# The pairs' weight sums: from sums on VectorE and GpSimd to transfers that add

## The chip, the cores and the metric

The kernel runs on one core of a Trainium2 chip. The core has five engines: TensorE (PE) multiplies matrices, VectorE (DVE) and ScalarE (ACT) work element by element, GpSimd (POOL) does general work and may issue transfers, and SyncE (SP) issues transfers. Sixteen DMA engines move data between DRAM and the on-chip memory. The metric is the time of one execution on the device in microseconds (us); less is better.

## What is computed

One layer of a hybrid sequence mixer over 16 learned tokens and 512 rows of width 2048, in float32:

```
u    = rms_norm(h, g_norm)
proj = u @ w_in                      # eight parts of 1024 columns: rq rk rv rg dq dk dv dg
r    = retention(rq, rk, rv)         # 8 heads of 128
r    = head_layer_norm(r) * silu(rg)
d    = diff_attention(dq, dk, dv)    # 8 heads, two softmaxes each
d    = head_rms_norm(d) * (1 - lam_init) * silu(dg)
out  = rms_norm(h + concat(r, d) @ w_out)
```

So each head needs eight column blocks of `w_in`, each 2048 x 128.

## The kernel before, in words

**Precision.** A float32 operand is split into a high part (rounded to the matmul's type by ScalarE) and a low part (operand minus high part, by VectorE). A product is then three matmuls: high x high, high x low, low x high.

**Start.** The rows of x are normalised, transposed and split into four quarters: `ua` (first half of the tokens, all 16 row tiles of D), `uc` and `ud` (second half, first and last eight row tiles). The first head's parts rv, rq, rk, rg, dv, dk are projected directly (`first_two`, `project`). Beside that, `sums_of_u` (L724 to L754) makes four signed sums of the quarters, `sums[1..4]`: `whole` joins high and low parts on GpSimd (L733), `out` splits a sum again (L736 to L738).

**Pairs.** The other 29 pairs of column blocks (`pair_list`: rv with rk, rq with rg, dv with dk, dq with dg) go through `run_pair`. A pair (ka, kb) is a product of a 2 x 2 block matrix of u with a 2 x 2 block matrix of weights: b11 and b21 are the two halves of ka, b12 and b22 those of kb, each 128 x 1024 in the buffer (512 KB). It is done with seven products in place of eight (Winograd's form of Strassen's scheme): P1 with b11, P2 with b21, P3 with b22, and four with sums of blocks: P7 with b22 - b12, P6 with b22 - b12 + b11, P5 with b12 - b11, P4 with b21 less the P6 sum. Each product is 24 matmuls (L813): 16 with the high part of the weights, 8 with the low part.

**Weights of a pair.** `load_pair` issues four loads (`raw_tile`, L94) into a ring of five buffers (`wr`). In DRAM a block's row is 128 numbers long, 512 B, so a load is 1024 pieces. `prepare_hi` copies the high part on ScalarE (L785), `prepare_lo` makes the low part on VectorE (L796) and then makes the next sum in place, over the buffer that was just read: after P3 on VectorE (L799), after P7 on VectorE (L801), after P1 two on GpSimd (L803, L804). The order of the products is P3, P7, P1, P6, P2, P5, P4. Product i runs while the parts of product i + 2 are prepared; there are three buffers each for high (`wh`) and low (`wl`) parts.

**Between the products** the work of heads that are already projected goes on by steps: `ret_task` (scores, decay, output), `diff_task` (two softmaxes per block, transposes, output), and `finish`, which normalises a head's output. In `finish` a row of sums goes by DMA over the partitions (`mc`, L467), through four small GpSimd steps (`rc`, L469 to L472), to DRAM (`rd`, L474) and back to all partitions (`sq`, L476); VectorE then multiplies (L479).

**Order.** After the start a scheduler of the framework orders the instructions of each engine at build time by its own estimate of durations; on the chip each engine works its list in order and waits on semaphores. A transfer belongs to the list of the engine that issues it: SyncE before the change, apart from the last stores.

**Output.** Five column chunks of `w_out` follow (L980 on), with the residual and the last norm.

Of the kernel before, what the change touches and what calls it, by code (L numbers as in the profile page):

```python
# [39 lines left out]
def hymba_kernel(ctx: ExitStack, tc: tile.TileContext, x, meta, norm_g, w_in, w_out, g_ret, g_diff,  # L40
# [27 lines left out]
    w_in_t, w_out_t = (w.rearrange("(k p) n -> p k n", p=P) for w in (w_in, w_out))  # L68

    def w_piece(name, h, half):  # L70
        c0 = OFFSETS[name] + h * P
        return w_in_t[:, half * 8:half * 8 + 8, c0:c0 + P]
# [622 lines left out]
    def put_dk(src):  # L695

        a = kbuf[0]
        for (d1, cols), (d2, _) in zip(*(both_parts(a[:, i, :]) for i in range(2))):
            act.copy(out=d1, in_=src[:, :, cols])
            vec.tensor_tensor(out=d2, in0=src[:, :, cols], in1=f(d1), op=ALU.subtract)  # L700
        return spread_dk()
# [22 lines left out]
    def sums_of_u():  # L724
# [3 lines left out]
        for k in range(0, 8, 2):  # L728
# [7 lines left out]
            def out(i, t):  # L736
                act.copy(out=sums[i][0][:, sl, :], in_=t)
                vec.tensor_tensor(out=sums[i][1][:, sl, :], in0=t, in1=f(sums[i][0][:, sl, :]), op=ALU.subtract)  # L738
# [3 lines left out]
            vec.tensor_tensor(out=d, in0=c, in1=d, op=ALU.add)  # L742
            out(1, d)
# [8 lines left out]
            vec.tensor_tensor(out=a2, in0=a2, in1=d, op=ALU.subtract)  # L752
            out(4, a2)
            yield  # L754

# [11 lines left out]
    ORDER = ("P3", "P7", "P1", "P6", "P2", "P5", "P4")  # L767
# [3 lines left out]
    def load_pair(n):  # L771
        if n < len(pair_list) and n not in raw_w:
            h, ka, kb = pair_list[n]
            raw_w[n] = {b: raw_tile(w_piece(k, h, half), P, f"{b}_{n}")
                        for b, k, half in (("b22", kb, 1), ("b12", kb, 0), ("b11", ka, 0), ("b21", ka, 1))}

    SOURCE = {"P3": "b22", "P7": "b22", "P1": "b11", "P6": "b22", "P2": "b21", "P5": "b12", "P4": "b11"}
# [10 lines left out]
    def prepare_lo(i):  # L788
# [9 lines left out]
        if pn == "P3":  # L798
            vec.tensor_tensor(out=w["b22"], in0=w["b22"], in1=w["b12"], op=ALU.subtract)  # L799
        elif pn == "P7":  # L800
            vec.tensor_tensor(out=w["b22"], in0=w["b22"], in1=w["b11"], op=ALU.add)  # L801
        elif pn == "P1":
            pool.tensor_tensor(out=w["b12"], in0=w["b12"], in1=w["b11"], op=ALU.subtract)  # L803
            pool.tensor_tensor(out=w["b11"], in0=w["b21"], in1=w["b22"], op=ALU.subtract)  # L804
# [11 lines left out]
    def run_pair(n, T):  # L816
# [19 lines left out]
        s37 = ap.tile([P, 2, HL], F32, tag="s37", name=f"s37_{nm}")[:, :, :w]  # L836
        p3 = pj(f"p3_{nm}")[:, :w]
        run(0, p3)
        snap(p3, None, s37[:, 0, :])
        step()  # L840
        v = pj(f"v_{nm}")[:, :w]
        run(1, v)
        snap(v, None, s37[:, 1, :])
# [276 lines left out]
```

## Time and profile before

| what | value |
|---|---|
| median of 3 runs | 1031.96 us (1031.91 to 1035.21) |
| the profiled execution | 1036.45 us |
| its span, first to last instruction | 1034.4 us |
| TensorE / VectorE / ScalarE / GpSimd busy | 93% / 80% / 52% / 23% of the span |
| mean granted clock of TensorE | 0.983 of full speed |
| transfers | 127.03 MB, mean 123 GB/s |

The page comes from the profiled execution. A busy share is an average over stages with different limits. Matmuls are pipelined, so a matmul's own duration (about 0.28 us) is longer than the distance to the next. Times in the trace count from the start of the span. Register, branch, semaphore and DMA-issuing instructions are not counted as busy.

### The profile page before, as it was taken

The page shows a single profiled execution, that of the slowest core. Times are in us where ns is not written, and L with a number is a line of the kernel's source. Part 1 is how long each engine was busy: PE and PEld are TensorE (multiplying, and loading weights), DVE is VectorE, ACT ScalarE, POOL GpSimd, SP SyncE. Part 2 cuts the span into 40 slices and gives each one's busy share as a digit, 9 for nine tenths or more (in the row PEclk, how much of TensorE's full clock was granted, in tenths as well). Part 3 has the DMA queues.
Part 4 walks back from the last instruction along what each step waited for, and adds up shares of the span by engine and source line. Part 5 has one row for each costly group of instructions (what it writes and reads, how often), then busy time and mean ns, then how long its engine had stood idle before and what let it go on. Part 6 is the DMA issues. An engine that isn't in the chain of part 4 may idle for free.

```text
span 1034.4 us, 18382 instructions
## 1 busy us (share of the span) xinstructions
PE 964.7 (93%) x7215; PEld 921.6 (89%) x7215; DVE 824.0 (80%) x1332; ACT 538.7 (52%) x979; POOL 242.7 (23%) x169
## 2 busy tenths in 40 slices
PE   6999988999999999899999999999994999799997
PEld 6999988999999999899999999999983988588896
DVE  6698869899989998999899989989996754334432
ACT  6454565565656564646565656565654443223322
POOL 4453131132233213321332133233220200000001
PEclk8999999999999999999999999999997999999998
DMA  9512533353235334543643264226443496143304
GB/s 269 158 43 73 125 93 103 82 155 114 82 97 152 107 109 116 139 121 87 140 134 98 82 156 113 83 82 156 113 113 102 161 385 212 50 126 96 122 1 163
DMA packets 166405, 127.03 MB, mean 123 GB/s; under 512 B 9712, under 2 KB 145008, under 8 KB 165808
## 3 DMA queue, kind: packets, MB, share of 16 engines
q1 hardware_dynamic: 165744, 124.04, 42.2%
q10 hardware_dynamic: 576, 1.84, 0.5%
q8 instruction: 56, 0.92, 0.4%
q14 instruction: 29, 0.24, 0.1%
HBM read 107.77 MB, written 11.57 MB: 115 GB/s over the span
## 4 chain that ended last, share of the span: by engine, by line
PE 54%; DVE 21%; DMA 9%; issue 6%; POOL 6%; ACT 4%; SPq 0%; POOLq 0%; DVEq 0%; ACTq 0%
PE y L526 6%; PE y L527 5%; PE y L528 5%; DVE wl_P L796 5%; PE y_rqrg L813 4%; PE x_dvdk L813 3%; PE x_dqdg L813 3%; DMA mc_r<-sq_r 2%; PE x_rqrg L813 2%; PE y_dvdk L813 2%; PE v_rqrg L813 2%; DMA sq_r<-rd_r 2%; PE v_dvdk L813 2%; DVE p_d L615 2%; PE y_rvrk L813 2%
## 5 line engine op out<-in xcount | busy, mean ns | idle before, releaser
L785 ACT CAST wh_P<-b 128x1024 fp32r<-128x1024 f32 x203 | 212.7, 1049 | 147.9 <-DVE mx_d L606 30.3
L796 DVE TENSOR_TENSOR wl_P<-b,wh_P 128x1024 fp32r<-128x1024 f32 x203 | 260.3, 1284 | 13.0 <-ACT wh_P L785 11.0
L803 POOL TENSOR_TENSOR b<-b,b 128x1024 f32<-128x1024 f32 x29 | 69.9, 2412 | 406.1 <-DVE b L799 301.7
L104 DVE TENSOR_TENSOR wl<-wr,wh 128x1024 fp32r<-128x1024 f32 (+1 forms) x40 | 49.8, 1252 | 69.3 <-ACT wh L103 69.2
L804 POOL TENSOR_TENSOR b<-b,b 128x1024 f32<-128x1024 f32 x29 | 76.8, 2649 | 105.5 <-DVE wl_P L796 32.5
L103 ACT CAST wh<-wr 128x1024 fp32r<-128x1024 f32 (+1 forms) x40 | 40.8, 1029 | 88.7 <-PE y L528 70.1
L607 ACT ACTIVATE p_d<-p_d,mx_d 128x144 f32<-128x144 f32 (+3 forms) x64 | 36.6, 572 | 31.7 <-DVE mx_d L606 31.1
L799 DVE TENSOR_TENSOR b<-b,b 128x1024 f32<-128x1024 f32 x29 | 35.5, 1223 | 0.6
L629 PE MATMUL at_d<-ident,p_d 128*128 128x128 f32 (+1 forms) x112 | 23.1, 275 | 13.3 <-DVE p_d L616 12.9
L801 DVE TENSOR_TENSOR b<-b,b 128x1024 f32<-128x1024 f32 x29 | 35.2, 1214 | 0.1
L813 PE MATMUL x_dqdg<-uah,wh_P 128*128 128x256 f32 x128 | 32.2, 290 | 3.0 <-ACT s_dqdg L825 3.0
L1049 POOL TENSOR_SCALAR rs<-ssq,pre 128x1 f32<-128x1 f32 x4 | 1.9, 486 | 136.1 <-ACT jk L1007 136.1
L813 PE MATMUL x_dqdg<-ual,wh_P 128*128 128x256 f32 x128 | 31.2, 282 | 0.0
L526 PE MATMUL y<-wh,mix_s3h 128*128 128x512 f32 (+1 forms) x64 | 23.6, 382 | 6.3 <-ACT mix_s3h L485 5.1
L813 PE MATMUL x_dvdk<-uah,wh_P 128*128 128x264 f32 x112 | 28.5, 284 | 0.0
L813 PE MATMUL x_dvdk<-ual,wh_P 128*128 128x264 f32 x112 | 28.4, 284 | 0.0
L813 PE MATMUL x_rvrk<-uah,wh_P 128*128 128x264 f32 x112 | 28.4, 285 | 0.0
L813 PE MATMUL x_rvrk<-ual,wh_P 128*128 128x264 f32 x112 | 28.2, 285 | 0.0
L629 PEld LDWEIGHTS at_d<-ident,p_d 128*128 128x128 f32 (+1 forms) x112 | 12.8, 126 | 17.3 <-DVE p_d L616 14.8
L813 PEld LDWEIGHTS x_dqdg<-uah,wh_P 128*128 128x128 f32 x128 | 24.1, 188 | 4.2 <-ACT s_dqdg L825 4.2
L526 PE MATMUL y<-wh,mix_s2h 128*128 128x512 f32 (+1 forms) x80 | 27.8, 348 | 0.0
L528 PE MATMUL y<-wh,mix_al 128*128 128x512 f32 (+1 forms) x80 | 27.8, 348 | 0.0
(567 smaller groups left out, 3550.5 us busy)
## 6 DMA issues: line engine op xcount, KB each, us to landing
b<-in_w_in_dram SPq DMA_DIRECT2D x116, 512.0 KB, 4.6
wr<-in_w_out_dram SPq DMA_DIRECT2D x32, 512.0 KB, 4.1
kbuf<-kbuf SPq DMA_DIRECT2D x24, 264.0 KB, 4.9
wr<-in_w_in_dram SPq DMA_DIRECT2D x12, 512.0 KB, 8.5
tab<-in_decay_tab_dram SPq DMA_DIRECT2D x8, 288.0 KB, 4.3
sq_r<-rd_r SPq DMA_DIRECT2D x8, 256.0 KB, 3.6
sq_d<-rd_d SPq DMA_DIRECT2D x8, 256.0 KB, 4.2
mx<-mxh_r SPq DMA_DIRECT2D x7, 256.0 KB, 3.7
```

The lines of the kernel that those rows point to most:

```text
L103: act.copy(out=hi, in_=raw)
L104: eng.tensor_tensor(out=lo, in0=raw, in1=f(hi), op=ALU.subtract)
L526: pe.matmul(o, ah, bh, start=start, stop=False)
L527: pe.matmul(o, ah, bl, start=False, stop=False)
L528: pe.matmul(o, al, bh, start=False, stop=stop)
L607: act.activation(p, p, AF.Exp, bias=mx, scale=slope, accum_out=zz[:, s:s + 1])
L629: pe.transpose(at[:n, b * P - q0:(b + 1) * P - q0], aa[b][:, kc:kc + n], ident)
L785: act.copy(out=hi, in_=raw_w[n][SOURCE[pn]])
L796: vec.tensor_tensor(out=lo, in0=w[SOURCE[pn]], in1=f(hi), op=ALU.subtract)
L803: pool.tensor_tensor(out=w["b12"], in0=w["b12"], in1=w["b11"], op=ALU.subtract)
L804: pool.tensor_tensor(out=w["b11"], in0=w["b21"], in1=w["b22"], op=ALU.subtract)
L813: pe.matmul(o, w_[:, kt, :], u[lo][:, kt, c0:], start=not add and w_ is wh and kt == 0 and lo == 0, stop=w_ is wl and kt == 7, skip_group_ ...
```

## The change

The four weight sums of a pair are no longer made by VectorE and GpSimd. GpSimd issues transfers that read a block of `w_in` from DRAM again and add it into the raw buffer (`more`, with `accum_op=ALU.add`). A transfer can add but not subtract, so all signs in the weights become plus: the buffer `t` starts as the first half of kb and has its second half added (P7), then the first half of ka (P6), then the second half of ka (P4), and b11 has the first half of kb added (P5). The signs move to where u and the results are split: `sums[1]` and `sums[4]` are negated, and so are the results rk, dk, rg and dg when they are copied or fed to Silu. P7 and P3 change places in the order, and `load_pair` for the next pair is called one product earlier. `w_in` lies in DRAM by blocks of 128 x 1024, so that a row of a piece is 4 KB long; the host lays it out before the launch.

```diff
--- before.py
+++ after.py
@@ -65,11 +65,11 @@
 
 
     pieces = []
-    w_in_t, w_out_t = (w.rearrange("(k p) n -> p k n", p=P) for w in (w_in, w_out))
+    w_out_t = w_out.rearrange("(k p) n -> p k n", p=P)
 
     def w_piece(name, h, half):
-        c0 = OFFSETS[name] + h * P
-        return w_in_t[:, half * 8:half * 8 + 8, c0:c0 + P]
+        r0 = (((OFFSETS[name] // P) + h) * 2 + half) * P
+        return w_in[r0:r0 + P, :].rearrange("p (k n) -> p k n", n=P)
 
     for name in ("rv", "rq", "rk", "rg", "dv", "dk"):
         for half in range(2):
@@ -696,8 +696,8 @@
 
         a = kbuf[0]
         for (d1, cols), (d2, _) in zip(*(both_parts(a[:, i, :]) for i in range(2))):
-            act.copy(out=d1, in_=src[:, :, cols])
-            vec.tensor_tensor(out=d2, in0=src[:, :, cols], in1=f(d1), op=ALU.subtract)
+            act.activation(d1, src[:, :, cols], AF.Copy, scale=-1.0)
+            vec.scalar_tensor_tensor(d2, src[:, :, cols], -1.0, f(d1), op0=ALU.mult, op1=ALU.subtract)
         return spread_dk()
 
     def spread_dk():
@@ -733,14 +733,15 @@
                 pool.tensor_tensor(out=t, in0=f(u[0][:, ks, :]), in1=f(u[1][:, ks, :]), op=ALU.add)
                 return t
 
-            def out(i, t):
-                act.copy(out=sums[i][0][:, sl, :], in_=t)
-                vec.tensor_tensor(out=sums[i][1][:, sl, :], in0=t, in1=f(sums[i][0][:, sl, :]), op=ALU.subtract)
+            def out(i, t, sign=1.0):
+                hi, lo = (x[:, sl, :] for x in sums[i])
+                act.activation(hi, t, AF.Copy, scale=sign)
+                vec.scalar_tensor_tensor(lo, t, sign, f(hi), op0=ALU.mult, op1=ALU.subtract)
 
             c = whole("fc", [t[k // 4] for t in uc], slice(k % 4, k % 4 + 2), "s2k", 3)
             d = whole("fd", ud, sl, "s2k", 3)
-            vec.tensor_tensor(out=d, in0=c, in1=d, op=ALU.add)
-            out(1, d)
+            vec.tensor_tensor(out=d, in0=c, in1=d, op=ALU.subtract)
+            out(1, d, -1.0)
             yield
             a1 = whole("fa", ua, sl, "sgd")
             vec.tensor_tensor(out=d, in0=d, in1=a1, op=ALU.subtract)
@@ -749,9 +750,10 @@
             a2 = whole("fb", ua, slice(8 + k, 10 + k), "tab")
             vec.tensor_tensor(out=c, in0=a1, in1=c, op=ALU.subtract)
             out(3, c)
-            vec.tensor_tensor(out=a2, in0=a2, in1=d, op=ALU.subtract)
-            out(4, a2)
+            vec.tensor_tensor(out=a2, in0=a2, in1=d, op=ALU.add)
+            out(4, a2, -1.0)
             yield
 
 
 
@@ -764,7 +766,7 @@
 
         ps_ = ps_[3:] if h == 0 else ps_[2:] + ps_[:2] if h == HEADS - 1 else ps_
         pair_list += [(h, *p_) for p_ in ps_]
-    ORDER = ("P3", "P7", "P1", "P6", "P2", "P5", "P4")
+    ORDER = ("P7", "P3", "P1", "P6", "P2", "P5", "P4")
     raw_w = {}
     split_w = {}
 
@@ -772,9 +774,15 @@
         if n < len(pair_list) and n not in raw_w:
             h, ka, kb = pair_list[n]
             raw_w[n] = {b: raw_tile(w_piece(k, h, half), P, f"{b}_{n}")
-                        for b, k, half in (("b22", kb, 1), ("b12", kb, 0), ("b11", ka, 0), ("b21", ka, 1))}
-
-    SOURCE = {"P3": "b22", "P7": "b22", "P1": "b11", "P6": "b22", "P2": "b21", "P5": "b12", "P4": "b11"}
+                        for b, k, half in (("t", kb, 0), ("b22", kb, 1), ("b11", ka, 0), ("b21", ka, 1))}
+            more(n, "t", kb, 1)
+
+    def more(n, b, name, half):
+
+        pool.dma_start(out=raw_w[n][b].rearrange("p (k n) -> p k n", n=P), in_=w_piece(name, pair_list[n][0], half),
+                       accum_op=ALU.add)
+
+    SOURCE = {"P7": "t", "P3": "b22", "P1": "b11", "P6": "t", "P2": "b21", "P5": "b11", "P4": "t"}
 
     def prepare_hi(i):
         n, j = divmod(i, 7)
@@ -795,13 +803,13 @@
         lo = wp.tile([P, 1024], F32R, tag="wl", bufs=3, name=f"wl_{n}_{pn}")
         vec.tensor_tensor(out=lo, in0=w[SOURCE[pn]], in1=f(hi), op=ALU.subtract)
         split_w[i].append(lo)
-        if pn == "P3":
-            vec.tensor_tensor(out=w["b22"], in0=w["b22"], in1=w["b12"], op=ALU.subtract)
-        elif pn == "P7":
-            vec.tensor_tensor(out=w["b22"], in0=w["b22"], in1=w["b11"], op=ALU.add)
+        _, ka, kb = pair_list[n]
+        if pn == "P7":
+            more(n, "t", ka, 0)
         elif pn == "P1":
-            pool.tensor_tensor(out=w["b12"], in0=w["b12"], in1=w["b11"], op=ALU.subtract)
-            pool.tensor_tensor(out=w["b11"], in0=w["b21"], in1=w["b22"], op=ALU.subtract)
+            more(n, "b11", kb, 0)
+        elif pn == "P6":
+            more(n, "t", ka, 1)
 
     def product(i, o, keys, add=False):
         pn = ORDER[i % 7]
@@ -834,19 +842,19 @@
             product(i0 + j, o, keys, more)
 
         s37 = ap.tile([P, 2, HL], F32, tag="s37", name=f"s37_{nm}")[:, :, :w]
+        v = pj(f"v_{nm}")[:, :w]
+        run(0, v)
+        snap(v, None, s37[:, 1, :])
+        step()
         p3 = pj(f"p3_{nm}")[:, :w]
-        run(0, p3)
+        run(1, p3)
         snap(p3, None, s37[:, 0, :])
-        step()
-        v = pj(f"v_{nm}")[:, :w]
-        run(1, v)
-        snap(v, None, s37[:, 1, :])
+        load_pair(n + 1)
         if keys:
             step()
         x = pj(f"x_{nm}")[:, :w]
         run(2, x)
         s1 = snap(x, "s1")
-        load_pair(n + 1)
         step()
         y = pj(f"y_{nm}")[:, :w]
         run(3, y)
@@ -874,7 +882,7 @@
             T[kb] = ap.tile([P, L], F32, tag="sg" + kb[0], name=f"sg_{kb}{h}")[:, :SEQ]
             for half in range(2):
                 add(T[kb][:, half * HS:half * HS + HS], su25, s37[:, half, :])
-            act.activation(T[kb], T[kb], AF.Silu)
+            act.activation(T[kb], T[kb], AF.Silu, scale=-1.0)
         else:
             for half in range(2):
                 add(s37[:, half, :], su25, s37[:, half, :])
@@ -882,8 +890,8 @@
             if kb == "rk":
                 T[kb] = [kbuf[0][:, i, :] for i in range(2)]
                 for (d1, cols), (d2, _) in zip(*(both_parts(t) for t in T[kb])):
-                    act.activation(d1, s37[:, :, cols], AF.Copy, scale=K_SCALE)
-                    vec.scalar_tensor_tensor(d2, s37[:, :, cols], K_SCALE, f(d1), op0=ALU.mult, op1=ALU.subtract)
+                    act.activation(d1, s37[:, :, cols], AF.Copy, scale=-K_SCALE)
+                    vec.scalar_tensor_tensor(d2, s37[:, :, cols], -K_SCALE, f(d1), op0=ALU.mult, op1=ALU.subtract)
             else:
                 T[kb] = put_dk(s37)
         run(6, v, True)
@@ -1089,7 +1097,8 @@
         ("x", a("x").reshape(SEQ, D)),
         ("meta", a("meta_tokens").reshape(META, 4, 512).transpose(1, 0, 2).reshape(4 * META, 512)),
         ("norm_g", a("norm_g").reshape(KT, P).T),
-        ("w_in", a("w_in").reshape(D, 8 * 1024)),
+
+        ("w_in", a("w_in").reshape(2, 8, P, 64, P).transpose(3, 0, 2, 1, 4).reshape(64 * 2 * P, 1024)),
         ("w_out", a("w_out").reshape(D, D)),
         ("g_ret", a("ret_norm_g").reshape(HEADS, P).T),
         ("g_diff", a("diff_norm_g").reshape(HEADS, P).T),
```

What the scheduler made of it, at two places. GpSimd, around the norm of a retention head (`rc_r`, `mc_r`; the first number in a block's name is the pair), before:

```order
L803 TENSOR_TENSOR b12_9_3881<-b12_9_3881,b11_9_3883 128x1024
L469 TENSOR_SCALAR rc_r2_3957<-mc_r2_3955 128x4
L470 TENSOR_TENSOR rc_r2_3957<-rc_r2_3957,mhalf_111 128x4
L471 TENSOR_SCALAR mc_r2_3955<-mc_r2_3955 128x4
L472 TENSOR_TENSOR rc_r2_3957<-rc_r2_3957,mc_r2_3955 128x4
L804 TENSOR_TENSOR b11_9_3883<-b21_9_3885,b22_9_3879 128x1024
L803 TENSOR_TENSOR b12_10_4215<-b12_10_4215,b11_10_4217 128x1024
L804 TENSOR_TENSOR b11_10_4217<-b21_10_4219,b22_10_4213 128x1024
```

and now:

```order
L782 DMA t_8_3533<-in_w_in_dram 128x1024
L782 DMA t_9_3848<-in_w_in_dram 128x1024
L782 DMA t_10_4160<-in_w_in_dram 128x1024
L469 TENSOR_SCALAR rc_r2_3958<-mc_r2_3956 128x4
L470 TENSOR_TENSOR rc_r2_3958<-rc_r2_3958,mhalf_111 128x4
L471 TENSOR_SCALAR mc_r2_3956<-mc_r2_3956 128x4
L472 TENSOR_TENSOR rc_r2_3958<-rc_r2_3958,mc_r2_3956 128x4
L782 DMA b11_9_3852<-in_w_in_dram 128x1024
L782 DMA t_9_3848<-in_w_in_dram 128x1024
L782 DMA t_10_4160<-in_w_in_dram 128x1024
L782 DMA t_11_4458<-in_w_in_dram 128x1024
L782 DMA b11_10_4164<-in_w_in_dram 128x1024
```

The two sums of a pair become four adds. An add of pair 10 stands between two of pair 9, and the adds of pair 9 stand ahead of and behind the four steps of `rc_r`.

SyncE at the same place, before:

```order
L94 DMA b22_10_4213<-in_w_in_dram 128x8x128
L467 DMA mc_r2_3955<-sq_r2_3810 128x1x4
L474 DMA rd_r2_3962<-rc_r2_3957 128x4
L476 DMA sq_r2_3810<-rd_r2_3962 128x512
L94 DMA b12_10_4215<-in_w_in_dram 128x8x128
L490 DMA mx2_4039<-mxh_r2_4035 128x512
L94 DMA b11_10_4217<-in_w_in_dram 128x8x128
L490 DMA mx2_4039<-mxl_r2_4036 128x512
L94 DMA b21_10_4219<-in_w_in_dram 128x8x128
```

and now:

```order
L467 DMA mc_r2_3956<-sq_r2_3809 128x1x4
L94 DMA b22_10_4162<-in_w_in_dram 128x1024
L474 DMA rd_r2_3963<-rc_r2_3958 128x4
L476 DMA sq_r2_3809<-rd_r2_3963 128x512
L490 DMA mx2_4039<-mxh_r2_4035 128x512
L94 DMA b11_10_4164<-in_w_in_dram 128x1024
L490 DMA mx2_4039<-mxl_r2_4036 128x512
L94 DMA b21_10_4166<-in_w_in_dram 128x1024
L94 DMA t_11_4458<-in_w_in_dram 128x1024
```

The load of b22 of the next pair has moved between `mc_r` and `rd_r`; the third load of a pair, b12, is gone, and the load of `t` stands first.

## Rows read from the trace of the kernel before

**Rows 1.** The page, part 1: busy time, share of the span and instructions.

```profile
span 1034.4 us, 18382 instructions
...
PE 964.7 (93%) x7215; PEld 921.6 (89%) x7215; DVE 824.0 (80%) x1332; ACT 538.7 (52%) x979; POOL 242.7 (23%) x169
```

**Rows 2.** Windows: stretch, length, each engine busy (instructions), TensorE clock, DMA share, GB/s.

```profile
core 0: us, PE busy (x) PEld busy (x) DVE busy (x) ACT busy (x) POOL busy (x), PEclk, DMA share, GB/s
100.00:755.00 655.00, 626.39 (x5039) 614.33 (x5038) 608.40 (x980) 391.00 (x704) 178.50 (x105) 1.00 0.43 113
755.00:800.00 45.00, 29.18 (x216) 26.75 (x215) 36.34 (x78) 24.11 (x49) 6.64 (x6) 0.85 0.39 104
950.00:1000.00 50.00, 50.00 (x297) 44.70 (x296) 18.47 (x22) 14.21 (x21) 0.00 (x0) 1.00 0.23 74
```

**Rows 3.** Waits of TensorE: waiting tile, releaser, us in all, times, longest.

```profile
PE at_d L629 <- DVE p_d L616: 12.9, 9, 2.1
PE y_rvrk L813 <- ACT s_rvrk L825: 9.3, 1, 9.3
PE s_d L590 <- DVE mx_d L604: 6.7, 5, 1.4
```

**Rows 4.** TensorE: chain (two heads), then timeline near 506 us: start, us, what.

```profile
310.93 2.94 PE x_dqdg L813 x24
...
505.88 2.94 PE x_dqdg L813 x24
...
505.72 0.36 PE L813 MATMUL x_dqdg<-uah,wh_P 128*128 128x256 f32 x1
```

**Rows 5.** The page, part 5: groups of the weight splits and sums.

```profile
L785 ACT CAST wh_P<-b 128x1024 fp32r<-128x1024 f32 x203 | 212.7, 1049 | 147.9 <-DVE mx_d L606 30.3
L796 DVE TENSOR_TENSOR wl_P<-b,wh_P 128x1024 fp32r<-128x1024 f32 x203 | 260.3, 1284 | 13.0 <-ACT wh_P L785 11.0
L803 POOL TENSOR_TENSOR b<-b,b 128x1024 f32<-128x1024 f32 x29 | 69.9, 2412 | 406.1 <-DVE b L799 301.7
...
L804 POOL TENSOR_TENSOR b<-b,b 128x1024 f32<-128x1024 f32 x29 | 76.8, 2649 | 105.5 <-DVE wl_P L796 32.5
...
L799 DVE TENSOR_TENSOR b<-b,b 128x1024 f32<-128x1024 f32 x29 | 35.5, 1223 | 0.6
```

**Rows 6.** Timeline of VectorE near 501 and 527 us, of GpSimd at 527 us.

```profile
501.23 1.21 DVE L796 TENSOR_TENSOR wl_P<-b,wh_P 128x1024 fp32r<-128x1024 f32 x1
...
526.95 0.42 DVE L693 SCALAR_TENSOR_TENSOR dq_h<-su_dqdg,dq_h 64x256 fp32r<-64x256 f32 x1
527.40 2.50 DVE L693 SCALAR_TENSOR_TENSOR dq_l<-su_dqdg,dq_l 64x256 fp32r<-64x256 f32 x1
...
526.99 2.64 POOL L804 TENSOR_TENSOR b<-b,b 128x1024 f32<-128x1024 f32 x1
```

**Rows 7.** Timeline from 793 to 800 us: VectorE, then TensorE.

```profile
793.61 0.69 DVE L479 TENSOR_TENSOR oc_d<-oc_d,sq_d 128x512 f32<-128x512 f32 x1 [4.37 <-DMA sq_d<-rd_d]
...
799.23 0.59 PE L813 MATMUL y_rvrk<-s2h,wh_P 128*128 128x264 f32 x1 [9.34 <-ACT s_rvrk L825]
```

**Rows 8.** DMA issues: count, KB each, median us from issue to landing.

```profile
b<-in_w_in_dram SPq DMA_DIRECT2D x116, 512.0 KB, 4.6
wr<-in_w_out_dram SPq DMA_DIRECT2D x32, 512.0 KB, 4.1
...
wr<-in_w_in_dram SPq DMA_DIRECT2D x12, 512.0 KB, 8.5
...
rd_r<-rc_r SPq DMA_DIRECT2D x8, 2.0 KB, 1.4
```

**Rows 9.** Groups of GpSimd: the power step in the pairs and at the start.

```profile
L470 POOL TENSOR_TENSOR rc_r<-rc_r,mhalf 128x4 f32<-128x4 f32 x8 | 10.9, 1363 | 0.7
...
L192 POOL TENSOR_TENSOR ss_x<-ss_x,mhalf 128x1 f32<-128x1 f32 x4 | 2.2, 554 | 0.3
```

## The prediction

> **What bounds the kernel now.** Read the busy shares first [rows 1]: TensorE 93% of the 1034.4 us span, VectorE 80%. The execution itself took 1036.45 us, 2.05 more than its span; the median of the runs, 1031.96, lies 4.5 us below it, so I add up against 1036.45 and name the result against the median at the end. The average hides stages, so read the windows next [rows 2]. Most of the 29 pairs lie from 100 to 755 us: 655 / 97.5 x 4 = 27 of them, by the head's length that follows. There VectorE is busy 608.4 of 655 us (93%) and TensorE 626.4 of 655 (96%): two engines are close to full together, and TensorE stands still for 28.6 us. From 755 to 800 us TensorE works 29.2 of 45 us, so 15.8 are lost. From 950 to 1000 us the pairs are over and VectorE is mostly free. The waits of TensorE [rows 3] say what ends its gaps: VectorE at most of them, and one gap of 9.3 us that belongs to the stretch 755 to 800. So the most that any relief of VectorE can give back is 28.6 + 15.8 us, whatever it takes off VectorE itself. Two heads' equal products stand at 310.93 and 505.88 us [rows 4]: 97.5 us a head, and with 28 products 3.48 us a slot, of which a product itself takes 2.94.
>
> **What goes.** Per pair two VectorE sums of 1.22 us (L799; L801 is the same form on the same sizes) and two GpSimd sums of 2.41 and 2.65 us [rows 5]: 29 x 2.44 = 71 us of VectorE, and all of GpSimd's 147 us of sums. The GpSimd passes cost VectorE time as well. From 526.99 to 529.63 us GpSimd runs one [rows 6]; the VectorE instruction that starts at 527.40 lasts 2.50 us where its twin just ahead of it took 0.42, and ends at 529.90, right after GpSimd. About 2 us of VectorE per GpSimd pass, 58 passes; not every pass catches an instruction so early, so I take 1.5 us and get about 87 us. Together some 158 us leave VectorE, 27/29 of it or 147 us in the first window. Its share there falls from 93% to (608 - 147) / 655 = 70%, and it no longer is the engine that others wait for. What is late next is TensorE itself, which had 4.4% left.
>
> How much of the 28.6 us comes back? Gaps that VectorE ended should close; the scheduler has put the program in a new order, though, with new places where a chain of softmax steps or a transfer ends last. I take two thirds, 19 us; bounds are 0 and 28.6. In 755 to 800 us a chain decides: VectorE waits 4.37 us for the transfer sq_d at 793.6, then TensorE starts at 799.23 after 9.34 us of nothing [rows 7]. That order stays, with two VectorE sums of 1.22 us and two GpSimd passes less ahead of it; I take 3 us, bounds 0 and 8. At the start the twelve loads of the first weights come in rows of 4 KB and no longer 512 B; they take 8.5 us to land where later ones take 4.6 [rows 8], all behind the loads of x. I take 1 us, bounds 0 and 3. The sign edits (scaled copies for plain ones, a scalar_tensor_tensor for a tensor_tensor, a scale in Silu) change no count: nothing, hidden under TensorE. Sum: 19 + 3 + 1 = 23 us, 1036.45 - 23 = 1013.
>
> **What comes.** Per pair four transfers of 512 KB that add, 116 in all, issued by GpSimd; loads stay four per pair. No row shows an adding transfer, so I bound its time from issue to landing. From below: a plain load of the same size in longer rows, 4.1 us. From above: the loads at the start, 8.5 us under full transfer engines, with a second whole load of 4.6 us behind: 13.1 us. I take 7 us: 4.1, and once more what 512 KB cost beyond a tiny transfer (4.1 - 1.4 = 2.7), since the buffer must be read as well [rows 8].
>
> What hides it is the distance in the new order. The low part of P7 must be made before the first column sum is added into t; P6 uses that, three products later; after P6's low part the second sum is added, and P4 uses it three products later again. Today the low part of P1 ends at 501.23 + 1.21 = 502.44 and its product begins at 505.72: a lead of 3.28 us [rows 4, 6], which I take for P7 too. From there to the start of P4's product there are 3.28 + 6 x 3.48 = 24.2 us. Off that go two high copies on ScalarE of 1.05 us and one low part of 1.28 on VectorE [rows 5], which leaves 20.8 us for two adds: **10.4 us each**. The add into b11 between P1 and P5 is a single link, 3.28 + 10.4 - 1.05 = 12.7 us. The first add, behind the load of t, has a whole pair of time, since t goes into the fifth buffer. At 7 us nothing waits, and the adds cost nothing; this is the cover the forecast rests on. Over 10.4 us every microsecond costs two per pair, 58 in all.
>
> Queues that the steps are moved past: GpSimd's queue runs in order, so an add that waits for a low part holds what stands behind it, the four small steps of rc, and rc that waits for mc holds the next adds. The old sums waited in the same places. On SyncE's queue b22 of the next pair now sits between mc and rd and waits for P4's low part, because it reuses the buffer of t. It must be there two slots later: 3.28 + 6.96 - 4.6 - 1.05 = 4.6 us to spare. If that load is late, rd and sq behind it are late, and VectorE stands at the gate product.
>
> **A rule against the change.** In this trace small GpSimd instructions are themselves held: the power step of rc takes 1363 ns in the pairs, where the same operation on one column took 554 ns at the start [rows 9]. I therefore allow an issue about 0.8 us of hold, inside the margin of 3.4. The Trainium skill, "SBUF — State Buffer", section "Who interferes with whom", goes further: a transfer issued from GpSimd can be starved of the time to write its descriptors while VectorE holds their shared ports. By that rule the time would be that of rival 2 below; the trace agrees that GpSimd is held, but shows no issue of this kind.
>
> **Rivals**, their times against the profiled execution where nothing else is said.
> 1. *Adding transfers are too slow* (slower). For: the transfer engines are 0.43 busy at 113 GB/s in the pairs [rows 2]. Adds bring 16 x 0.524 MB per 97.5 us, 86 GB/s more. At the price of long rows (0.23 for 74 GB/s, from 950 to 1000 us, so 0.0031 per GB/s) that gives 0.43 + 0.27 = 0.70; counted twice because the buffer is read too, 0.96. At 0.96 transfers queue as at the start, where a load took 8.5 us; with the 2.7 us of the second read an add takes 11.2 us, 0.8 over the margin: 0.8 x 58 = 46 us, less the 23 of gain, 1036 + 23 = 1059. At the upper bound of 13.1 it would be 1170. Against: long rows make the loads cheaper as well. It decides from 10.4 us on. 18%.
> 2. *GpSimd is held while it issues* (slower). If an issue is held by VectorE for 4 us, an add takes 7 + 4 = 11 us: 0.6 x 58 = 35, less 23, 1048. Against: VectorE at 70% leaves gaps. It decides from 3.4 us of hold on. 8%.
> 3. *The relief is taken back* (no change, or little). VectorE gets free, but TensorE's gaps come from chains: the scores wait in order for softmax steps, sq lands late behind b22, and each head loses what it lost. Then 0 to 6 of the 23 us come: 1026 to 1032 against the runs. For: TensorE is 96% busy from 100 to 755 us already. Against: the gaps end mostly on VectorE [rows 3]. 14%, of which 6 go to faster by over 0.3% and 8 to no change.
> 4. *The change doesn't do what it says*: the adds might not take the place of all four sums. The order has 58 rows fewer on VectorE, and on GpSimd 116 adds for 58 sums, so I give this nothing.
>
> **How the numbers follow.** The forecast, 60%: 1013 against the profiled execution, 1009 against the runs, whose middle lies 4.5 us lower; I name **1009 us**. Its own range runs from 1000 (28.6 + 4 us back) to 1026 (a quarter back). The range of all cases, 998 to 1070, takes in rival 3, rival 2 and the nearer part of rival 1; left out is what lies above, some 12%, and 3% below. A measurement of this kernel can tell 0.3%, 3 us, from no change. Faster: 60 + 6 = 0.66. No change: 0.08. Slower: 18 + 8 = 0.26.
>
> **What would show it right or wrong.** Right: VectorE 68 to 75% busy from 100 to 750 us, no instruction of it stretched to 2 us and more, TensorE at 98%, adds landing in 6 to 9 us, transfer engines 0.6 to 0.8 busy. Rival 1: adds landing after 11 us, ScalarE's high copies of P6, P4 and P5 waiting for transfers, engines over 0.9. Rival 2: landing late though the transfer engines are free, with long issues on GpSimd. Rival 3: VectorE freed, TensorE's idle time unchanged, now ended by scores or by sq. The forecast is wrong if the pairs still take 97 us a head.

## The result: 1.058 times the time before, and the profile after

The changed kernel takes 1092.67 us (median of 4 runs, 1088.99 to 1098.35), the kernel before 1032.77 us beside it: a ratio of 1.0581, 95% interval 1.0531 to 1.0631. The forecast was 1009 us, range 998 to 1070. It missed the sign. The ratios below leave out one slow run, of e7 (1065 us).

The page of the changed kernel, busy times, transfers and queues:

```profile
span 1090.3 us, 18493 instructions
...
PE 986.8 (91%) x7215; PEld 945.3 (87%) x7215; DVE 673.2 (62%) x1274; ACT 532.8 (49%) x979; POOL 186.4 (17%) x227
...
DMA packets 68423, 187.88 MB, mean 172 GB/s; under 512 B 11568, under 2 KB 15792, under 8 KB 67824
...
q1 hardware_dynamic: 51056, 124.04, 35.4%
q0 software_dynamic: 16704, 60.82, 31.5%
...
L782 POOL DMA_DIRECT2D t<-in_w_in_dram x87 | 76.5, 919 | 547.0 <-DVE wl_P L804 137.5
...
L804 DVE TENSOR_TENSOR wl_P<-t,wh_P 128x1024 fp32r<-128x1024 f32 x87 | 106.2, 1222 | 66.4 <-ACT wh_P L793 63.8
...
t<-in_w_in_dram POOLq DMA_DIRECT2D x87, 512.0 KB, 6.5
b<-in_w_in_dram SPq DMA_DIRECT2D x87, 512.0 KB, 5.2
...
b<-in_w_in_dram POOLq DMA_DIRECT2D x29, 512.0 KB, 7.0
```

Against [rows 1] the relief came nearly as announced: VectorE 824.0 to 673.2 us, 151 less for some 158 forecast. TensorE has the same 7215 matmuls but takes 22 us longer over them, and its idle time grew from 69.7 to 103.5 us (span less busy). The adds are the queue q0, and land in 6.5 and 7.0 us (medians; the longest of the 116 in 10.1).

The windows, columns as in [rows 2]:

```profile
100.00:755.00 655.00, 600.34 (x4679) 590.42 (x4678) 431.72 (x850) 354.51 (x648) 117.78 (x145) 0.96 0.77 181
755.00:800.00 45.00, 37.68 (x290) 36.62 (x289) 32.49 (x70) 26.05 (x50) 8.00 (x11) 0.92 0.84 199
```

In 655 us TensorE does 4679 matmuls in place of 5039, at a granted clock of 0.96 in place of 1.00. The transfer engines are 0.77 busy.

Who ends the waits of TensorE (as [rows 3]), then those of ScalarE and VectorE:

```profile
PE y_dqdg L821 <- ACT s_dqdg L833: 31.5, 6, 6.0
PE y_rvrk L821 <- ACT s_rvrk L833: 23.4, 5, 8.7
PE x_rvrk L821 <- ACT s_rvrk L833: 7.5, 2, 5.2
...
ACT wh_P L793 <- DMA t<-in_w_in_dram: 84.1, 27, 6.0
ACT sq_r L454 <- DVE oc_d L479: 28.4, 7, 4.9
...
DVE oc_d L479 <- DMA sq_d<-rd_d: 59.0, 8, 9.3
DVE oc_r L479 <- DMA sq_r<-rd_r: 46.7, 8, 12.4
```

Before, VectorE ended most gaps; now ScalarE's copies of partial products do (s_dqdg, s_rvrk). ScalarE takes its work in order, and two things stand ahead of these copies: high copies that wait for an add into t, and the squares of finish (L454), which wait for VectorE, which stands at L479 for sq. One head shows both. The timeline of the changed kernel, engine by engine (start, us, engine, line, what):

```profile
420.88 0.51 SPq L467 DMA_DIRECT2D mc_d<-sq_d  x1
427.78 0.33 SPq L474 DMA_DIRECT2D rd_d<-rc_d  x1
428.23 0.42 SPq L94 DMA_DIRECT2D b<-in_w_in_dram  x1
434.13 0.33 SPq L476 DMA_DIRECT2D sq_d<-rd_d  x1
...
423.36 1.75 POOL L782 DMA_DIRECT2D t<-in_w_in_dram  x2 [15.39 <-DMA t<-in_w_in_dram]
425.19 0.94 POOL L469 TENSOR_SCALAR rc_d<-mc_d 128x4 f32<-128x4 f32 x1
...
429.88 0.68 DVE L450 TENSOR_SCALAR oc_r<-o_r 128x512 f32<-128x512 f32 x1
438.85 0.69 DVE L479 TENSOR_TENSOR oc_d<-oc_d,sq_d 128x512 f32<-128x512 f32 x1 [8.28 <-DMA sq_d<-rd_d]
...
433.36 1.05 ACT L793 CAST wh_P<-t 128x1024 fp32r<-128x1024 f32 x1 [4.96 <-DMA t<-in_w_in_dram]
434.31 0.36 ACT L833 COPY s_dqdg<-v_dqdg 128x256 f32<-128x256 f32 x1
439.58 0.63 ACT L454 ACTIVATE sq_r<-oc_r 64x512 f32<-64x512 f32 x1 [4.90 <-DVE oc_d L479]
440.11 1.03 ACT L793 CAST wh_P<-b 128x1024 fp32r<-128x1024 f32 x1
441.05 0.36 ACT L833 COPY s_dqdg<-p_dqdg 128x256 f32<-128x256 f32 x1
...
441.46 0.58 PE L821 MATMUL y_dqdg<-s2h,wh_P 128*128 128x256 f32 x1 [5.09 <-ACT s_dqdg L833]
```

The four adds of a pair are named here by what they add: kb1, ka0 and ka1 go into t (for P7, P6 and P4), b11 is the one into the buffer b11 (for P5); ka0 and ka1 are called the two links. GpSimd stands 15.39 us for the load of t, then issues two adds back to back (kb1 of the next pair, ka0 of this one). Only behind them come finish's steps. rd, 2 KB, goes out at 427.78, with a plain load of 512 KB right behind it (428.23), and lets sq go at 434.13, when the adds have landed too. VectorE waits for sq until 438.85. oc_r was ready at 430.56, yet ScalarE's sq_r waits for L479: oc, sq and sr share three buffers, and the free one is sq_d's. The copy s_dqdg stands behind it, and TensorE loses 5.09 us. The same four steps of a head in the kernel before:

```profile
494.68 0.51 SPq L467 DMA_DIRECT2D mc_d<-sq_d  x1
501.17 0.34 SPq L474 DMA_DIRECT2D rd_d<-rc_d  x1
502.79 0.33 SPq L476 DMA_DIRECT2D sq_d<-rd_d  x1
...
507.89 0.69 DVE L479 TENSOR_TENSOR oc_d<-oc_d,sq_d 128x512 f32<-128x512 f32 x1 [1.17 <-DMA sq_d<-rd_d]
```

The windows of the stretch in the changed kernel:

```profile
424.00:428.00 4.00, 4.00 (x35) 4.00 (x35) 2.91 (x7) 1.96 (x6) 3.52 (x6) 1.00 0.80 141
428.00:432.00 4.00, 4.00 (x36) 4.00 (x35) 2.57 (x5) 0.40 (x1) 0.94 (x1) 1.00 1.06 215
432.00:436.00 4.00, 4.00 (x36) 4.00 (x35) 0.00 (x0) 1.32 (x2) 0.00 (x0) 1.00 1.02 266
436.00:440.00 4.00, 0.37 (x4) 0.14 (x2) 1.15 (x2) 0.42 (x1) 0.00 (x0) 1.00 0.70 184
440.00:444.00 4.00, 2.54 (x12) 2.54 (x13) 4.00 (x5) 3.83 (x7) 0.89 (x1) 0.54 0.39 44
444.00:448.00 4.00, 4.00 (x24) 3.98 (x24) 1.33 (x4) 1.18 (x2) 0.00 (x0) 0.61 0.98 263
448.00:452.00 4.00, 4.00 (x36) 3.95 (x35) 3.91 (x5) 2.80 (x6) 0.00 (x0) 1.00 1.00 362
```

While rd is under way the transfer engines are full (1.06, 1.02). After the gap the granted clock is 0.54 and 0.61 for two windows, mostly the lower level of 1.2 GHz. On the busy time there that costs 2.54 x 0.46 + 4.00 x 0.39 = 2.7 us on top of the 5.09.

### The profile page after: what moved, and what is told of

It is laid out like the page before. It is cut to its first block, busy times and chain, and to the rows that moved or that the text cites. A ratio compares the mean times of both kernels' runs of the same rounds, so it can differ in the third digit from the quotient of the medians.

```text
span 1090.3 us, 18493 instructions
## 1 busy us (share of the span) xinstructions
PE 986.8 (91%) x7215; PEld 945.3 (87%) x7215; DVE 673.2 (62%) x1274; ACT 532.8 (49%) x979; POOL 186.4 (17%) x227
## 4 chain that ended last, share of the span: by engine, by line
PE 49%; DMA 27%; DVE 9%; POOL 5%; issue 4%; ACT 4%; SPq 0%; POOLq 0%; ACTq 0%; DVEq 0%
DMA t<-in_w_in_dram 12%; PE y L526 5%; PE y L527 5%; PE y L528 5%; PE y_rvrk L821 4%; DMA sq_r<-rd_r 4%; DMA rd_r<-rc_r 3%; DVE wl_P L804 3%; PE v_rqrg L821 3%; DMA rd_d<-rc_d 3%; PE x_rqrg L821 3%; DMA sq_d<-rd_d 2%; PE y_rqrg L821 2%; PE y_dqdg L821 2%; PE p_rqrg L821 2%
## 5 line engine op out<-in xcount | busy, mean ns | idle before, releaser
L782 POOL DMA_DIRECT2D t<-in_w_in_dram x87 | 76.5, 919 | 547.0 <-DVE wl_P L804 137.5
L793 ACT CAST wh_P<-b 128x1024 fp32r<-128x1024 f32 x116 | 121.4, 1046 | 95.6 <-issue 21.9
L804 DVE TENSOR_TENSOR wl_P<-b,wh_P 128x1024 fp32r<-128x1024 f32 x116 | 141.6, 1221 | 37.6 <-ACT wh_P L793 33.8
L793 ACT CAST wh_P<-t 128x1024 fp32r<-128x1024 f32 x87 | 90.9, 1048 | 131.6 <-DMA t<-in_w_in_dram 84.1
L804 DVE TENSOR_TENSOR wl_P<-t,wh_P 128x1024 fp32r<-128x1024 f32 x87 | 106.2, 1222 | 66.4 <-ACT wh_P L793 63.8
L821 PE MATMUL y_dqdg<-s2h,wh_P 128*128 128x256 f32 x64 | 24.5, 393 | 31.5 <-ACT s_dqdg L833 31.5
L821 PEld LDWEIGHTS y_dqdg<-s2h,wh_P 128*128 128x128 f32 x64 | 18.4, 287 | 33.0 <-ACT s_dqdg L833 33.0
L821 PE MATMUL y_rvrk<-s2h,wh_P 128*128 128x264 f32 x56 | 21.5, 395 | 23.4 <-ACT s_rvrk L833 23.4
L479 DVE TENSOR_TENSOR oc_d<-oc_d,sq_d 128x512 f32<-128x512 f32 x8 | 5.5, 692 | 59.0 <-DMA sq_d<-rd_d 59.0
L782 POOL DMA_DIRECT2D b<-in_w_in_dram x29 | 26.6, 917 | 78.6 <-DVE wl_P L804 37.4
L479 DVE TENSOR_TENSOR oc_r<-oc_r,sq_r 128x512 f32<-128x512 f32 x8 | 5.5, 693 | 46.7 <-DMA sq_r<-rd_r 46.7
L821 PE MATMUL x_dqdg<-ual,wh_P 128*128 128x256 f32 x128 | 31.3, 283 | 0.0
L821 PEld LDWEIGHTS x_rvrk<-uah,wh_P 128*128 128x128 f32 x112 | 22.2, 198 | 8.0 <-ACT s_rvrk L833 7.9
L821 PE MATMUL x_rqrg<-uah,wh_P 128*128 128x256 f32 x112 | 28.0, 287 | 1.2 <-ACT s_rqrg L833 1.2
```

Source lines behind the costliest of these rows:

```text
L479: vec.tensor_tensor(out=oc, in0=oc, in1=bc, op=ALU.mult)
L782: pool.dma_start(out=raw_w[n][b].rearrange("p (k n) -> p k n", n=P), in_=w_piece(name, pair_list[n][0], half), accum_op=ALU.add)
L793: act.copy(out=hi, in_=raw_w[n][SOURCE[pn]])
L804: vec.tensor_tensor(out=lo, in0=w[SOURCE[pn]], in1=f(hi), op=ALU.subtract)
L821: pe.matmul(o, w_[:, kt, :], u[lo][:, kt, c0:], start=not add and w_ is wh and kt == 0 and lo == 0, stop=w_ is wl and kt == 7, skip_group_ ...
```

## The experiments

Theories at the start: **the chain** (finish's mc, rc, rd, sq arrive later behind the adds), **the late adds** (ScalarE's high copies wait for them), **plain traffic** (61 MB more), **the order** (new order and signs cost by themselves). Ratios are to the kernel before on the same chip (1038 to 1041 us there), with 95% intervals.

**e1: the block layout alone**, put on the kernel before.

```diff
-        return w_in_t[:, half * 8:half * 8 + 8, c0:c0 + P]
+        return w_in[r0:r0 + P, :].rearrange("p (k n) -> p k n", n=P)
```

> The kernel before with input weights by blocks in DRAM, and its sums on VectorE and GpSimd as they were. All theories: VectorE still bounds (93% busy in 100 to 755 us), packets fall from 166405 to about 60000 and the loads land sooner (median below 4.6 us), time 1022 to 1035 us. Should the block layout be what slows the small transfers of finish, the time would be 1050 or more and rd would wait over 4 us to land.

1031.65 us, ratio 0.9921 (0.9895 to 0.9946). Packets fall to 51717, loads land in 4.2 us. This is the fastest complete version here: it beats both kernels.

**e2: no adds. e3: the adds become writes.**

```diff
-        pool.dma_start(out=raw_w[n][b]..., in_=w_piece(...), accum_op=ALU.add)
+        pass                                                      # e2
+        pool.dma_start(out=raw_w[n][b]..., in_=w_piece(...))      # e3
```

> The changed kernel with the 116 adding DMAs left out, so that the products run on wrong weights; copies, differences, loads, signs and order stay. If the adds cost the time (by their landing, or by what they do to other transfers): 1000 to 1015 us, PE 97% busy in the pairs, rd landing in about 1.5 us again. If the new order of the products (P7 ahead of P3), the signs or the queue order of the loads cost it: 1060 us or more.

> The changed kernel with its 116 POOL transfers to the same buffers at the same places, but writing in place of adding, so that the sums are left out; every wait and every byte stays. If reading and writing back in the buffer is what is dear: transfers land in 4 to 5 us in place of 6.5 to 7, and the time falls to 1030 to 1060 us. If the bytes and the place in the queues are what counts: 1080 to 1095 us, as with the adds.

e2: 1030.95 us, 0.9916 (0.989 to 0.9942), equal to e1. The windows of e1, then of e2:

```profile
100.00:755.00 655.00, 630.45 (x5085) 618.34 (x5085) 612.27 (x989) 394.58 (x709) 166.48 (x105) 1.00 0.40 115
```

```profile
100.00:755.00 655.00, 634.04 (x5086) 625.66 (x5085) 476.69 (x939) 394.20 (x712) 23.29 (x52) 0.99 0.41 116
```

136 us less of VectorE and 143 less of GpSimd move TensorE by one matmul. Taking out the sums and bringing in the new order and signs are together worth nothing. That each is worth nothing by itself is not shown: TensorE's waits at at_d fell from 9.4 us in e1 to 2.8 in e2, and those at s_d rose from 6.9 to 19.3.

e3: 1042.72 us, 1.0036 (1.0011 to 1.0062). Its instructions stand in the same order on every engine as in the changed kernel; only the kind of 116 transfers differs. Its queue and its transfers from the page, then its waits of TensorE:

```profile
q0 software_dynamic: 16704, 60.82, 19.1%
...
t<-in_w_in_dram POOLq DMA_DIRECT2D x87, 512.0 KB, 4.6
```

```profile
PE y_dqdg L820 <- ACT s_dqdg L832: 16.1, 6, 4.0
PE y_rvrk L820 <- ACT s_rvrk L832: 13.2, 4, 8.6
PE x_rvrk L820 <- ACT s_rvrk L832: 1.8, 3, 0.7
```

So the bytes and their places cost 12 us against e2 (whose order differs), and adding in place of writing costs the rest. The two spans differ by 1090.3 - 1041.1 = 49.2 us: TensorE's busy time by 986.8 - 970.4 = 16.4 at the lower clock (busy time times mean granted clock is alike: 986.8 x 0.957 = 944, 970.4 x 0.971 = 942), its idle time by 32.8, of which the three waits above make 15.4 + 10.2 + 5.7 = 31.3.

**e4: nobody waits for sq at L479** (the norm is left out). **e8: mc, rc, rd and sq left out too.**

```diff
-        vec.tensor_tensor(out=oc, in0=oc, in1=bc, op=ALU.mult)
+        vec.tensor_scalar(oc, oc, 1.0, -1.0, op0=ALU.min, op1=ALU.max)
```

> The changed kernel with the product of oc and the broadcast factor (L479) replaced by a clamp of oc alone of the same shape, so that the norm is left out of the heads' result; the transfers mc, rd and sq still run, and nobody waits for them. If VectorE and ScalarE standing at L479 and L454 behind the slower small transfers are the loss (16 chains, each 4 us longer than before): 1030 to 1050 us. If the late adds at ScalarE's high copies are the loss: 1080 us or more, with wh_P still waiting 85 us or more for t and b.

> The changed kernel with mc, rc, rd and sq left out altogether and oc clamped in place of multiplied, so that the norm is left out of the heads' result and no buffer is held by those transfers. If the small transfers of finish, each 4 us later behind the adds, are the loss: 1050 us or less. If the adds at ScalarE's high copies are: 1075 us or more, with wh_P still waiting 75 us or more for t.

e4: 1086.25 us, 1.0456 (1.041 to 1.0502). It did not cut the chain. Waits of ScalarE and TensorE in e4:

```profile
ACT sr_r L455 <- DMA sq_d<-rd_d: 65.3, 7, 11.4
...
PE y_dqdg L821 <- ACT s_dqdg L833: 38.8, 5, 8.6
```

The wait moved from L479 to ScalarE, whose sr_r takes the buffer that sq_d is still landing in. e8: 1041.23 us, 1.0022 (0.999 to 1.0053), with all adds in and ScalarE waiting longer for them than in the change:

```profile
ACT wh_P L781 <- DMA t<-in_w_in_dram: 97.7, 24, 9.1
```

So with all the adds, late as they are, but without finish's transfers the kernel stands 1041 - 1031 = 10 us above e2, and with them 1099 - 1031 = 68 (e9 below). e2 still has finish's transfers; a kernel without these and without the adds was not run, and the order of the engines moved in e8 too. So this says where the loss passes, not to the microsecond.

**e5: only the two links** (ka0, ka1); **e6: only kb1 and b11**; **e7: as e6, the links on VectorE**; **e10: b11 left out**; **e11: kb1 on VectorE**; **e12: all three sums of t on VectorE.**

```diff
-            more(n, "t", kb, 1)        # e5 drops it; e11, e12: t + b22 on VectorE ahead of P7's copy
-            more(n, "t", ka, 0)        # e6 drops it; e7, e12: t + b11 on VectorE
-            more(n, "b11", kb, 0)      # e5, e10 drop it
-            more(n, "t", ka, 1)        # e6 drops it; e7, e12: t + b21 on VectorE
```

> The changed kernel with the add of kb1 into t ahead of P7 and the add into b11 after P1 left out (sums missing); the two adds into t between P7, P6 and P4 stay, 58 of 116. If the late landing of these two, in front of ScalarE's high copies, is the loss: it stays almost whole, 1070 us or more, and wh_P waits over 50 us for t. If the loss goes with the bytes and the engines' load: about half is left, 1050 to 1068 us.

> The other half: the adds of kb1 into t and into b11 stay, the two between P7, P6 and P4 are left out (sums missing). If the two links are the loss: 1030 to 1045 us, wh_P waits under 20 us for t and b. If the loss goes with the bytes: 1050 to 1068 us, as with the other half.

> Nothing left out: the adds of kb1 and into b11 by DMA, the two sums into t between P7, P6 and P4 by VectorE from b11 and b21, which lie in the buffers anyway (58 sums of about 1.2 us, 71 us of VectorE); GpSimd has no passes. If the two links are the loss: 1028 to 1042 us, VectorE 75 to 80% busy in the pairs and no instruction stretched. If the loss goes with the bytes: 1050 to 1068 us.

> The changed kernel itself beside the others on one chip: 1090 to 1100 us, the ratio to before again 1.05 to 1.065.

> The changed kernel with the add into b11 after P1 alone left out (29 of 116; its sum is missing); ScalarE, VectorE and PE keep their order but for a few instructions. If each add costs alike, a quarter of the loss over before goes: 1078 to 1085 us. If the add of kb1, which POOL issues back to back with that of ka0 just when finish's rd is due, is the loss: 1085 us or more. If it is the add into b11 that keeps a transfer in flight at rd: 1060 us or less.

> Nothing left out: t + kb1 is made by VectorE from b22, which lies in its buffer anyway (29 sums of 1.2 us), the other 87 adds by DMA. If the pair of adds kb1 and ka0 at finish's rd is the loss: 1030 to 1045 us, and rd's landing falls from 5.5 us towards 3. If the number of bytes counts: 1075 to 1085 us.

> Nothing left out: the three sums into t by VectorE (87 of 1.2 us, VectorE 80% busy in the pairs), only the 29 adds into b11 by DMA. All theories: 1028 to 1042 us, no better than the block layout alone (0.992 of before), since with no sums at all the time was the same.

e5 1030.66 us, 0.991 (0.9875 to 0.9945). e6 1069.11, 1.0292 (1.0261 to 1.0322). e7 1053.85, 1.0115 (1.0064 to 1.0166). e9, the change again, 1099.03, 1.059 (1.0557 to 1.0623). e10 1084.27, 1.0422 (1.0389 to 1.0456). e11 1071.12, 1.0307 (1.0278 to 1.0337). e12 1065.63, 1.0259 (1.0234 to 1.0283).

The late adds as such fall with e5: both links are in, ScalarE waits 36.8 us for t, and nothing is lost. But e6 with equal bytes lies 38 us above it, which none of the theories said. Two of TensorE's waits are longer in e6: that at y_dqdg, 18.4 us against 5.0, and that at s_d for the softmax's mx_d, 24.8 us in e6. Leaving a transfer out makes the scheduler order the engines anew (only e10 kept nearly all of the change's order), so these runs mix two causes. In e11 VectorE stands 33.9 us at the new sum for the load of b22. Why e12 loses 27 us with 29 adds is not settled; **e15** asked whether b22's buffer is to blame.

```diff
-        r = wp.tile([P, 1024], F32, tag="wr", bufs=5, name=nm)
+        r = wp.tile([P, 1024], F32, tag="wt" if t else "wr", bufs=2 if t else 3, name=nm)
```

> The kernel with only the 29 adds into b11 by DMA and three sums by VectorE (1066 us with five buffers in rotation), with two buffers of its own for t and three for b22, b11, b21, so that b22 of the next pair takes b22's buffer, free after P3, in place of t's, free after P4. If the late load of b22 was what 29 adds cost: 1030 to 1042 us. If not: 1060 us or more, and the adds or the order of the products are what costs.

1063.52 us, 1.0226 (1.0183 to 1.0268): it is not. TensorE's largest gaps in the pairs there, as in e12, are 5 to 6 us at y_rvrk in two heads, beside one of 8.2 us near 825 us that e1 has too (8.8). e12 and e15 run the new order of the products with most sums on VectorE, so what that order costs stays open.

**e13, e14: rd and sq replaced by two matmuls**, in the changed kernel and in e1.

```diff
-        nc.sync.dma_start(out=rd, in_=rc)
-        nc.sync.dma_start(out=bc, in_=rd...broadcast_to([P, SEQ]))
+        vec.scalar_tensor_tensor(sq..., i4, float(P), r4, op0=ALU.mult, op1=ALU.mult)
+        act.copy(out=sh, in_=sq)
+        vec.tensor_tensor(out=dl, in0=sq, in1=f(sh), op=ALU.subtract)
+        pe.matmul(bc, ones, sh, start=True, stop=False)
+        pe.matmul(bc, ones, dl, start=False, stop=True)
```

> The changed kernel, nothing left out, with rd and sq (to DRAM and back, spread over 128 partitions) replaced by two matmuls of ones with a diagonal of the factors (high and low part, two VectorE instructions and one ScalarE copy more for each finish); all 116 adds stay. If the chain behind the adds is the loss: it shortens from 17.5 to 9 to 12 us, PE's wait at y_dqdg goes, and the time is 1040 to 1065 us, with 10 to 20 us of it the price of the remedy. If the late adds at the high copies are the loss by themselves: 1085 us or more.

> The same remedy in the kernel before with the block layout, which has no adds. Its chain of 13 us was hidden, so only the remedy's price shows: 1031 to 1048 us. Should it fall under 1025, the chain was not hidden before either.

e13 1110.4 us, 1.0676 (1.0651 to 1.0701); e14 1076.64, 1.0349 (1.0323 to 1.0375). The remedy itself costs 45 us where no add is (0.9921 to 1.0349), of which TensorE stands 16.8 + 7.9 us in order for the diagonal's high copy; the expectations allowed at most 20. Over its own base the adds cost 1.0676 - 1.0349, 34 us, in place of 1.059 - 0.9921, 69 us, and the wait at y_dqdg falls to 9.4 us. It agrees with the chain as about half of the loss, but the order changed too, and TensorE now stands 30.6 us at bc_r (7.9 in e14).

**e16 to e18: same order, same bytes, only the kind of each transfer differs** (writing, `ALU.bypass`, where not adding; those sums are left out).

```diff
+            more(n, "t", kb, 1, ALU.add)      # e16, e18
+            more(n, "t", ka, 0, ALU.add)      # e17, e18
+            more(n, "b11", kb, 0, ALU.add)    # e16
+            more(n, "t", ka, 1, ALU.add)      # e17
```

> The changed kernel with the same 116 transfers in the same order, adding at kb1 and into b11, writing at ka0 and ka1 (those sums are left out). If the loss is each add's own late landing at the next high copy: little, 1043 to 1055 us, since kb1 and b11 have the most time. If it is the engine time that an add takes from whatever else is under way: about half of the 56 us, 1062 to 1080 us.

> The same with adding at ka0 and ka1 and writing at kb1 and into b11. If the late landing at the copies of P6 and P4 is the loss: 1080 us or more, wh_P waits 70 us or more for t. If it is engine time: about half, 1062 to 1080 us. If an add is harmless alone and the two back to back (kb1, ka0) count: under 1060 us.

> The same with adding at kb1 and ka0 and writing at ka1 and into b11. If the two adds in flight at finish's rd are the loss, through the chain that is 12.4 us too long for PE: 1075 us or more, rd landing in 5 to 6 us and the d chains 17 us long. If the links are: 1060 to 1075 us. If engine time: 1062 to 1080 us, the chains 16 to 17 us.

e16 1068.36 us, 1.0282 (1.0258 to 1.0306); e17 1069.66, 1.0295 (1.0259 to 1.033); e18 1078.18, 1.0373 (1.0338 to 1.0409). Over e3 (1.0036) that is 26, 27 and 35 us for 58 adds each, and 57 for all 116 (e9). Halves that share no add (e16, e17) sum to 53: the price goes with the adding, some 0.45 us each in either half. The pair at finish is dearer (0.6), but does not carry the whole, as e18 was to show. Where it strikes is read from the d chain (from SyncE's mc_d to VectorE's L479, in the timeline) and TensorE's wait at y_dqdg, means of the six middle heads in us; e5 and e6 have orders of their own:

```
kernel          mc to rd   rd to sq   chain    wait at y_dqdg   chain less wait, each head
before          6.2        2.0        12.7     none             (10.2 to 14.1)
e3 all write    6.1        3.5        15.3     2.7              12.3 to 12.9
e17 links add   6.7        5.1        16.7     4.1              12.4 to 12.9
e10 no b11      8.0        5.2        17.3     4.7              12.3 to 12.9
e18 pair adds   8.0        5.2        17.4     4.7              12.4 to 12.9
e16 slack add   6.7        4.6        17.9     5.3              12.3 to 12.9
the change      8.1        5.2        17.9     5.2              12.3 to 12.9
e9 (again)      8.0        5.5        18.5     5.8              12.3 to 12.9
e5 links alone  5.6        4.0        13.7     0.8              12.9
e6 kb1 and b11  5.5        4.1        15.5     3.1              12.4 to 12.9
```

In 42 heads of the change's order (e10's is all but the same) the wait is the chain less 12.3 to 12.9 us: that order has room for a chain of 12.6, and each microsecond over it is one of TensorE. e5, which lost nothing, has chains that almost fit. In the kernel before the chain was 12.7 (10.2 to 14.1) and TensorE did not wait there. The rest is at the rvrk products, where the r chain and a late add meet (at 464.15 in the head above ScalarE waits 4.61 us for t, at 469.31 VectorE has waited 2.78 for sq_r), and in the clock. e4 fits: its wait at y_dqdg stayed.

Between e3 and the change, in one and the same order, the chain grows by 2.6 us: 2.0 ahead of rd and 1.7 from rd to sq, while sq's own part gives back 1.1. Ahead of rd mc lands 0.7 us later, and GpSimd is late: the issue of an add takes it 0.92 us, that of a write 0.54, and the four steps of rc stand behind such issues, in every second head also between them (changed kernel, GpSimd):

```profile
533.25 0.54 POOL L469 TENSOR_SCALAR rc_d<-mc_d 128x4 f32<-128x4 f32 x1
533.85 0.88 POOL L782 DMA_DIRECT2D t<-in_w_in_dram  x1
534.45 1.37 POOL L470 TENSOR_TENSOR rc_d<-rc_d,mhalf 128x4 f32<-128x4 f32 x1
```

How much an add costs through the 16 transfer engines and how much through GpSimd, no run here separates.

The times of e2, e5, e11, e12 and e14 lie outside every range that their expectations named, that of e6 by 1 us. Those of e4 and e13 lie in the range named for the late adds as the loss; but e4 did not cut the chain, and in e13 the 45 us of the remedy hide what it gave back.

## Why the prediction was wrong, step by step

**What goes: the amounts right, the gain wrong.** VectorE fell to 431.7 / 655 = 66% (70 forecast; 476.7 / 655 = 73% in e2, which keeps the pace), and its low parts take 1222 ns in place of 1284 [rows 5]. "I take two thirds, 19 us": measured nothing, e2 against e1, with the new order in it. That is what rival 3 said: with all sums gone TensorE waits 19.3 us at s_d for the softmax's mx_d. That VectorE ended the gaps [rows 3] need not mean that its load made them; a chain that passes through VectorE ends there too.

**The block layout: mis-sized.** "I take 1 us": e1 measures 0.8%, 7 to 8 us. I priced only the loads at the start; in 100 to 755 us TensorE's idle time fell from 28.6 [rows 2] to 24.5. Where the rest lies is open.

**The add's time: right.** 7 us taken, 6.5 and 7.0 measured; engines 0.77 busy (0.70 to 0.96 worked out in rival 1).

**"At 7 us nothing waits, and the adds cost nothing": the step that failed.** At the same order the adding itself costs some 57 us (e9 against e3). The step has two faults. ScalarE did wait, 84 us at 27 copies, though no add took over 10.4 us to land: GpSimd's order put kb1 of the next pair, waiting for its load, ahead of ka0, so an add was issued late, and two at once. I named the order of that queue and then wrote that the old sums had waited in the same places. Such waits alone cost little, as far as e8 (98 us of them) and e5 (37 us) show in orders of their own. The second fault is larger: I priced an add by who waits for its own result, and not by what else is on the engines meanwhile. On SyncE I asked whether b22 would be late in front of rd and sq; the queue did let rd go, and the chain grew at two other places. From rd to sq it takes 5.2 us, where the kernel before took 2.0 in the same heads (rd_d's median landing: 2.2 before, 4.5 now; the 1.4 of [rows 8] is rd_r's). From mc to rd it takes 8.1 in place of 6.2, on GpSimd's queue, whose order I had named. Nor did I ask how much the chain might grow, though [rows 7] show such a wait of 4.37 us ending in a gap of 9.34.

**Clock: left out.** Gaps of 5 us lowered it, 16.4 us of the 49 between e3 and the change; gaps of up to 2.1 us in the pairs of the kernel before had not (1.00 in [rows 2]).

**Rivals.** Rival 1 had the sign and 1059 us, but by adds of 11 us on engines over 0.9; neither came, though its third sign did, ScalarE's high copies of P6 and P4 waiting for transfers. Rival 2: an issue takes 0.92 us, the longest 1.19, so no hold of 4 us; that an add takes longer to issue than a write (0.54) stood in no rival. Here the rule of the Trainium skill, "SBUF — State Buffer", section "Who interferes with whom", that descriptor writing can be starved by VectorE, did not show; VectorE was at 66%. My sign that GpSimd is held, 1363 against 554 ns [rows 9], compared four columns with one: in e2, with neither sums nor adds, the step still takes 1038 to 1044 ns. The forecast gave 12% to what lies above 1070.

## What to carry to other kernels

Before moving sums to transfers, take the sums out and time that: where nothing is gained, as here, there is little to win by moving them. Price a transfer by what it takes from all others, on the transfer engines and in the queue that issues it, and look first at the smallest transfers on a serial chain and at the in-order engine that waits for them. Compare variants at equal instruction order, by changing the kind of a transfer and not its presence; two variants here with equal bytes and unequal order lay 38 us apart (e5, e6).

## What the runs showed of the hardware

- An adding transfer of 512 KB takes the 16 engines 0.315 x 1090.3 / 116 = 2.96 us, a writing one 0.191 x 1041.1 / 116 = 1.71 us: 1.7 times, with 6.5 against 4.6 us to landing.
- Issuing an adding transfer keeps GpSimd busy 0.92 us, a writing one 0.54 (e3).
- A transfer of 2 KB issued while two adds are under way, with a plain load right behind it, lands when they have landed: 5.96 us in the head shown; rd_d's median is 2.2 us in the kernel before, 3.2 among writes (e3), 4.5 in the change.
- After a gap of 5.09 us TensorE's granted clock was 0.54 and 0.61 over the next two windows of 4 us; between e3 and the change the clock added half of what the idle time did (16.4 to 32.8 us).
- Beside finish's transfers the 116 transfers cost 12 us as writes (e3 against e2) and 68 as adds (e9 against e2); with finish's transfers left out the kernel with all adds lies 10 us above e2 (e8, in another order).
